# An expert's first weights used in two halves by all its passes, in the MoE of a transformer block

## The chip, the cores and the metric

One core of a Trainium2 chip. Its engines run side by side and meet at semaphores: TensorE (PE in the rows; PEld its weight loads, PEq its sequencer), VectorE (DVE), ScalarE (ACT), GpSimd (POOL), and SyncE (SP), which here mainly issues DMA transfers. PSUM is the memory that TensorE accumulates in, SBUF the working memory. The metric is device time of one execution in microseconds (us), lower is better.

## The reference

One streaming-encoder block on 256 tokens of width 1024: layer norm, one wide projection, a sparse latent attention and a state-space mixer, merged, and then a mixture of experts. All of the change lies in the last part:

```python
logits = (xt @ w_router + b_router)
top_val, top_idx = lax.top_k(logits, 4)            # 4 of 32 experts for each of 256 tokens
gates = jax.nn.softmax(top_val, axis=-1)
# for every expert e, for the tokens that chose it, with their gates g:
h = xt[tok] @ w1[e] + b1[e]                        # w1[e] is 1024 x 2048, float32
gate, up = h[:, :1024], h[:, 1024:]
gate = jnp.minimum(gate, 7.0); up = jnp.clip(up, -7.0, 7.0)
act = (up + 1.0) * gate * jax.nn.sigmoid(1.702 * gate)
acc.at[tok].add((act @ w2[e] + b2[e]) * g[:, None])   # w2[e] is 1024 x 1024
```

The 32 experts' weights are 384 MB in float32, all of them read once.

## The kernel before

The first quarter of the time goes to attention and mixer; from about 375 us on the kernel loops over the 32 experts (L1637 of the program). The order of instructions on each engine is the order in which the code is written.

**Weights.** An expert's weights are 12 units of 1 MB, eight of w1 (128 rows of 1024 each) and four of w2. They pass through a ring of 17 tiles (names wa, wb, wc; load_unit, L1014). SP issues the loads in order: load_more(8) after the block "a" of an expert and load_more(4) after its block "b". A load waits for the last matmul that reads the old contents of its tile, so when the ring is full it is TensorE that gives a tile back. The transfers are issued from one queue, in order.

**Slots and passes.** The tokens of an expert are numbered in slots. Pass 0 computes the first 32 slots for every expert; pass 1 the slots 32 to 63, pass 2 slots 64 to 127, pass 3 slots 128 to 191. Passes 1 to 3 stand in nested tc.If blocks on the number of tokens (if_more), which every engine branches around where they aren't needed (TensorE at L1508). With this input pass 1 runs in twelve experts (3, 6, 8, 10, 15, 16, 17, 21, 24, 27, 28, 30), pass 2 in experts 3, 15 and 17, and pass 3 in expert 15. `will` places a hint ahead of a branch for TensorE's instruction fetch.

**One expert.** Pass 0 takes its tokens from xg, gathered an expert pair ahead; its first product (first_bias and first_mm) goes through the eight w1 units into the PSUM tile X[0]. Then comes block "a": for each further pass the whole first product over the same eight units (more_first; passes 2 and 3 gather their own tokens with 32 matmuls into xo), swiglu on VectorE and ACT, one-hot matrices for the scatter (slots), and transposes (turn). Then the previous expert's outputs are scattered into acc (the list late), the next pair's tokens are gathered, pass 0's result is transposed, and its second product goes through the four w2 units into X[1] and Y[1]. Block "b" does the second product of the further passes (more_second) and scatters it: for each half of the columns ACT writes yh, the rounded scaled value, VectorE yl, the remainder, and eight matmuls add both into acc.

**Buffers.** go and so (swiglu of further passes), yh and yl of further passes, and some late scratch share a rotation of four tiles of 2 KB per partition (wide, tag t2k). h of a 64-slot pass lies in Y[0] and X[1].

In the last expert, w2 is loaded in column halves, and the residual and final layer norm follow each half.

Of the kernel before, what the change touches and what calls it, by code (L numbers as in the profile page):

```python
# [64 lines left out]
def shape_constants():  # L65
    p = np.arange(P)
    f32 = np.float32
    ident = np.eye(P, dtype=f32)
    tri = (p[:, None] <= p[None, :]).astype(f32)
    tgt = (p[:, None] > p[None, :]).astype(f32)  # L70
    trs = (p[:, None] < p[None, :]).astype(f32)
    iota = np.tile(np.concatenate([p % 32 + 1, p % 64 + 1, p + 1]).astype(f32)[None, :], (P, 1))
# [20 lines left out]
def kernel(ctx, tc, A, out, dbg=None):  # L93
# [43 lines left out]

    cst = const.tile([P, 672], F32, name="cst")
    nc.scalar.dma_start(cst[:, 0:128], A["cst"][:, 0:128])
# [261 lines left out]
    def small_b():  # L401
        small(cst2, A["cst"][:, 672:1184])
        small(cst3, A["cst"][:, 1184:1568])
        small(cst[:, 128:672], A["cst"][:, 128:672])
# [1020 lines left out]

    def first_mm(w, x, h, m, k):
        for c in range(4):
            t, j = h[c * m // P], c * m % P
            mm(t[j:j + m, :], lhsT=x[:, k, 0:m], rhs=w[:, :, c * 256:c * 256 + 256], start=False,  # L1429
               stop=(k == KD - 1), skip_group_check=True)  # L1430

    def turn(us, h, a):
        for i, u in enumerate(us):
            for c in range(2):
                tr(h[i][:, cut(c)], u[:, cut(c)], ident)
            act(a[:, i * 256:i * 256 + 256], h[i][:, 0:256], AF.Copy)  # L1436

# [11 lines left out]

    def scale_y(y, gs, tag=None):  # L1450
        v = [wide(nm, F32R) if tag else buf(nm, [512], F32R, 2) for nm in ("yh", "yl")]
        act(v[0], y, AF.Copy, scale=gs)  # L1452
# [21 lines left out]

    def own_gather(e, base):
        g = buf("hgo", [2, M])
        onehot(g, e, iota64[:, 0:M], base)
        gather(g, xo, 0, X[1], M)

    def more_first(e, p):  # L1480
# [12 lines left out]
        turn(us, h, aTs[p])  # L1493

    def more_second(e, p, nhs):
# [5 lines left out]
        for nh in nhs:  # L1501
            scatter(nh, more[e, p][0], scale_y(ys[nh], more[e, p][1], "t2k"))

# [11 lines left out]
    def rest(e, dw):  # L1515
        own_gather(e, FULL)
        sg = slots(e, put_hot(e, iota64, FULL, "o"), Y[1], "2", 1)
        h, a = (X[0], Y[0]), aTs[2]
        first_bias(e, h, M)
        for k in range(KD):  # L1520
            nc.sync.dma_start(dw, w1[e, cut(k), :])
            first_mm(dw.rearrange("p (g c) -> p g c", g=2), xo, h, M, k)
        turn([swiglu(t, True) for t in h], h, a)
        y = X[1], Y[1]
# [6 lines left out]
        for nh in range(2):  # L1531
            scatter(nh, sg[0], scale_y(y[nh], sg[1], "t2k"))

    def gate_values():
        for tt in range(2):
            m8 = rm8[:, tt, :]
            nm = buf("rnm", [4], bufs=2)
            V.tensor_scalar(nm[:, 0:1], m8[:, 0:1], -1.0, None, op0=OP.mult)
            ex = buf("rex", [NE], bufs=2)
            act(ex, l36[:, tt, 0:NE], AF.Exp, bias=nm[:, 0:1])  # L1540
# [4 lines left out]
        dump("gates", gates)  # L1545
        gr = buf("gr", [2, NE])
        V.tensor_copy(gp[:, :, :, 0], gates)
# [7 lines left out]
    def res(tt, hf, eng):  # L1555
        cs = slice(hf * 512, (hf + 1) * 512)
        tmp = wide("ftmp")
        V.tensor_tensor(tmp, acc[tt][hf], fin[0][:, cs], op=OP.mult)  # L1558
# [78 lines left out]
    for e in range(NE):  # L1637
# [113 lines left out]
```

## Time and profile before

| | before |
|---|---|
| median of 3 runs | 1521.28 us (1519.26 to 1521.94) |
| profiled execution, its own time | 1524.34 us |
| span of that execution in the trace | 1522.5 us |
| TensorE busy | 1225.6 us (80% of the span) |
| VectorE, ACT, POOL busy | 35%, 19%, 11% |
| mean granted TensorE clock | 0.905 of full |
| read from HBM | 475 MB |

The share of busy time is a mean over stretches that differ. A wait in the rows names what ended last before an instruction; an instruction's duration includes its overlap with its neighbours, since matmuls are pipelined.

### The profile page before, as it was taken

The numbers are of one execution on the slowest core, as the hardware profiler recorded it, in microseconds if no ns is written. First come the engines' busy times: TensorE is split into PE (matmuls) and PEld (weight loads), VectorE is DVE, ScalarE is ACT, GpSimd is POOL, SyncE is SP. The second block draws the span as 40 slices with busy tenths as digits, with TensorE's granted clock in tenths as the row PEclk, the third lists the DMA queues.
The fourth block names the chain that finished last, engine by engine and source line by source line (L and its number), as shares of the span: only waits on it lengthen the run. The fifth ranks groups of instructions, "written<-read, shape, count | busy, mean of one in ns | idle before, by whom it ended". The sixth has DMA issues, their size and how long they took to land. (4 is left out here: it accounts for less than half of the span.)

```text
span 1522.5 us, 21278 instructions
## 1 busy us (share of the span) xinstructions
PE 1225.6 (80%) x8399; PEld 666.2 (44%) x8399; DVE 537.1 (35%) x1107; ACT 294.1 (19%) x508; POOL 172.1 (11%) x123
## 2 busy tenths in 40 slices
PE   6988989998768878787777788988867777778784
PEld 3778778886323333334323243433332323323331
DVE  5678689786311212122212112221121212212134
ACT  2465546543100101010100001011000001001011
POOL 2333135423000000000000000000000000000002
PEclk9889989999978999899998869989998989989896
DMA  9777446987995699999999905465899999999971
GB/s 305 227 216 255 159 161 203 307 290 304 372 409 220 245 414 415 412 412 415 413 413 414 407 31 221 193 252 215 323 415 415 412 414 415 414 413 370 386 316 43
DMA packets 127430, 480.89 MB, mean 316 GB/s; under 512 B 12635, under 2 KB 49643, under 8 KB 92406
## 3 DMA queue, kind: packets, MB, share of 16 engines
q1 hardware_dynamic: 122598, 472.40, 79.3%
q10 hardware_dynamic: 4624, 5.67, 1.2%
q8 instruction: 137, 2.24, 0.6%
q14 instruction: 71, 0.58, 0.1%
HBM read 475.00 MB, written 3.03 MB: 314 GB/s over the span
## 5 line engine op out<-in xcount | busy, mean ns | idle before, releaser
L1429 PE MATMUL px<-wb,xg 128*32 128x512 f32 x1080 | 143.1, 646 | 28.4 <-DMA wb<-in_w 24.4
L1459 PE MATMUL acc<-yh,sT 128*128 128x512 f32 x192 | 95.4, 497 | 50.2 <-PEq L1508 39.5
L1395 POOL TENSOR_TENSOR xg<-xg,modT 128x512 f32<-128x512 f32 x32 | 33.3, 1040 | 875.9 <-DVE xg L1393 875.9
L1412 DVE TENSOR_SCALAR gu<-px 128x256 f32<-128x256 f32 x32 | 13.6, 425 | 303.5 <-PE px L1429 303.5
L426 PE MATMUL pj<-uTh,wl 128*128 128x256 f32 x360 | 106.9, 297 | 5.4 <-DVE wl L305 2.9
L426 PE MATMUL pj<-uTh,wh 128*128 128x256 f32 x360 | 108.6, 302 | 0.4 <-ACT iqz L645 0.4
L305 POOL TENSOR_TENSOR wl<-wa,wh 128x1024 fp32r<-128x1024 f32 x34 | 87.8, 2583 | 178.6 <-ACT wh L304 150.4
L426 PE MATMUL pj<-uTl,wh 128*128 128x256 f32 x360 | 106.4, 295 | 0.0
L1453 DVE SCALAR_TENSOR_TENSOR yl<-px,gs,yh 128x512 fp32r<-128x512 f32 x48 | 36.0, 751 | 198.1 <-ACT yh L1452 194.2
L304 ACT ACTIVATE wh<-wa 128x1024 fp32r<-128x1024 f32 x75 | 78.7, 1057 | 107.3 <-PE pj L426 77.7
L1459 PE MATMUL acc<-yl,sT 128*128 128x512 f32 x192 | 92.7, 483 | 4.5 <-DVEq L1508 3.1
L1414 ACT ACTIVATE sgm<-gu 128x256 f32<-128x256 f32 x32 | 13.3, 416 | 397.0 <-DVE gu L1412 397.0
L1459 PEld LDWEIGHTS acc<-yh,sT 128*128 128x128 f32 x192 | 43.6, 227 | 97.1 <-issue 54.1
L1429 PEld LDWEIGHTS px<-wb,xg 128*32 128x32 f32 x1080 | 34.6, 115 | 116.3 <-issue 68.4
L1443 PE MATMUL px<-wb,aT 128*32 128x512 f32 (+1 forms) x376 | 70.3, 600 | 17.0 <-ACT aT L1436 8.9
L1429 PE MATMUL px<-wa,xg 128*32 128x512 f32 x504 | 73.3, 685 | 11.4 <-DMA wa<-in_w 8.8
L1393 DVE TENSOR_TENSOR xg<-py,sc 128x512 f32<-128x512 f32 x32 | 22.1, 692 | 170.1 <-PE py L1389 99.0
L426 PEld LDWEIGHTS pj<-uTh,wl 128*128 128x128 f32 x360 | 72.6, 202 | 8.2 <-POOL wl L305 3.5
L1389 PEld LDWEIGHTS py<-hg,n 128*128 128x128 f32 x512 | 71.1, 213 | 11.2 <-issue 6.2
L426 PEld LDWEIGHTS pj<-uTh,wh 128*128 128x128 f32 x360 | 72.7, 202 | 4.0 <-issue 2.9
L1389 PE MATMUL py<-hg,n 128*128 128x128 f32 x512 | 69.8, 294 | 5.5 <-issue 2.5
L1429 PE MATMUL px<-wc,xg 128*32 128x512 f32 x464 | 62.8, 656 | 13.4 <-DMA wc<-in_w 13.4
(442 smaller groups left out, 2069.2 us busy)
## 6 DMA issues: line engine op xcount, KB each, us to landing
wb<-in_w SPq DMA_DIRECT2D x201, 1024.0 KB, 19.1
wc<-in_w SPq DMA_DIRECT2D x92, 1024.0 KB, 20.1
wa<-in_w SPq DMA_DIRECT2D x91, 1024.0 KB, 18.4
wa<-in_w_in SPq DMA_DIRECT2D x24, 1024.0 KB, 6.9
wa<-in_w_mod SPq DMA_DIRECT2D x16, 1024.0 KB, 5.0
wa<-in_w_mod SPq DMA_DIRECT2D x16, 512.0 KB, 6.1
wa<-in_w_proj_b SPq DMA_DIRECT2D x4, 1024.0 KB, 5.2
wa<-in_w_proj_a SPq DMA_DIRECT2D x4, 1024.0 KB
```

The source lines that it names most:

```text
L304: i = act(xh, x, AF.Copy)
L305: eng.tensor_tensor(xl, x, xh.bitcast(F32), op=OP.subtract)
L426: mm(o, lhsT=a[:, k, :], rhs=b[:, k, :], start=(k == 0 and i == 0), stop=(k == KD - 1 and i == 2), skip_group_check=True)
L1389: mm(t[:, i * m:(i + 1) * m], lhsT=n2[:, tt, cut(k0 + i)], rhs=oh[:, tt, :], start=(tt == 0), stop=(tt == 1), skip_group_check=True)
L1393: V.tensor_tensor(o, t.rearrange("p (a s) -> p a s", a=n), sc2[:, ks].unsqueeze(2).to_broadcast([P, n, m]), op=OP.mult)
L1395: G.tensor_tensor(o, o, sh2[:, ks].unsqueeze(2).to_broadcast([P, n, m]), op=OP.add)
L1412: V.tensor_scalar(gt, h[:, 0:w], SWIGLU_LIMIT, None, op0=OP.min)
L1414: act(sg, gt, AF.Sigmoid, scale=SWIGLU_ALPHA)
L1429: mm(t[j:j + m, :], lhsT=x[:, k, 0:m], rhs=w[:, :, c * 256:c * 256 + 256], start=False, stop=(k == KD - 1), skip_group_check=True)
L1443: mm(y[m * j:m * j + m, :], lhsT=a[:, b:b + m], rhs=w, start=(k < n), stop=(k >= KD - n), skip_group_check=True)
L1453: V.scalar_tensor_tensor(v[1], y, gs, v[0].bitcast(F32), op0=OP.mult, op1=OP.subtract)
L1459: mm(acc[tt][nh], lhsT=sT[:, tt, :], rhs=y, start=False, stop=False, skip_group_check=True)
```

## The change

w1 of an expert is used in two halves of four units. After pass 0's first four units comes a block "a0", in which every further pass goes over the same four; then load_more(4) gives SP those four tiles; then pass 0's last four units, a block "a1" with the further passes over them, and load_more(4). Pass 1 keeps its sums in its PSUM tile Y[0] between the blocks. The 64-slot passes share X[1] and Y[1], so they copy their sums of the first half into a new SBUF tile, part, and add it to the sums of the second half before swiglu. Each such pass keeps its gathered tokens (tiles xa2, xa3, later reused for the transposed result).

The rotation t2k is gone: go and so, and yho and ylo for the second product of all further passes, are single tiles; scratch of the end lies in part. hp, hg and sT of pass 0 go from two buffers to one. In the last expert pass 0's second product is scaled ahead of the branch, and the final rows are built after block "a1".

```diff
-    def wide(nm, dt=F32):
-        return buf(nm, [512], dt, 4, "t2k")
-
     def act_tiles(spare):
-        return (wide("go"), wide("so")) if spare else (buf("gu", [512]), buf("sgm", [256]))
+        return (buf("go", [512]), buf("so", [256])) if spare else (buf("gu", [512]), buf("sgm", [256]))
-    aTs = {1: buf("aT1", [256]), 2: buf("aT2", [512]), 3: buf("aT3", [512])}
-    xo = buf("xo", [KD, M])
+    aTs = {1: buf("aT1", [256]), 2: buf("xa2", [512]), 3: buf("xa3", [512])}
+    part = {2: buf("part2", [2, 512]), 3: buf("part3", [2, 512])}
+    yo = [buf(nm, [512], F32R) for nm in ("yho", "ylo")]
...
+    def more_first(e, p, q):
+        ks = range(4 * q, 4 * q + 4)
         if p == 1:
-            put = put_hot(e, iota32, T, "o")
-            x, h, m = xs(e)[:, :, T:M], (Y[0],), T
+            x, h, m, k0 = xs(e)[:, :, T:M], (Y[0],), T, -1
         else:
-            put = put_hot(e, iota64, LOW[p], "o")
-            own_gather(e, LOW[p])
-            x, h, m = xo, (Y[0], X[1]), M
-        first_bias(e, h, m)
-        for k in range(KD):
-            first_mm(wt[e * 12 + k], x, h, m, k)
-        us = [swiglu(t, True) for t in h]
-        more[e, p] = slots(e, put, Y[1], str(p), 1)
-        turn(us, h, aTs[p])
+            x, h, m, k0 = own(p), (X[1], Y[1]), M, 4
+            if q == 0:
+                own_gather(e, LOW[p], x)
+        if q == 0:
+            first_bias(e, h, m)
+        else:
+            put = put_hot(e, iota32 if p == 1 else iota64, LOW[p], "o")
+        for k in ks:
+            first_mm(wt[e * 12 + k], x, h, m, k, k0)
+        if p > 1:
+            v = [part[p][:, i, :] for i in range(2)]
+            if q == 0:
+                V.tensor_copy(v[0], h[0])
+                act(v[1], h[1], AF.Copy)
+            else:
+                for i in range(2):
+                    V.tensor_tensor(v[i], h[i], v[i], op=OP.add)
+        if q == 1:
+            for i, t in enumerate(h):
+                u = swiglu(v[i] if p > 1 else t, True)
+                if i == 0:
+                    more[e, p] = slots(e, put, Y[1], str(p), 1)
+                turn(u, X[1] if p > 1 else t, aTs[p], i)
...
-            scatter(nh, more[e, p][0], scale_y(ys[nh], more[e, p][1], "t2k"))
+            scatter(nh, more[e, p][0], scale_y(ys[nh], more[e, p][1], yo))
...
-        will(e, "a")
+        will(e, "a0_")
         first_bias(e, (h,), T)
         for k in range(KD):
             first_mm(wt[e * 12 + k], xs(e), (h,), T, k)
...
-        us = [swiglu(h)]
-        if_more(e, "a", more_first)
-        load_more(KD)
+            if k == 3:
+                if_more(e, "a0_", more_first, 0)
+                load_more(4)
+                will(e, "a1_")
+        u = swiglu(h)
+        if_more(e, "a1_", more_first, 1)
+        load_more(4)
...
             second_mm(w2_part(e, k, nh), y[nh], aT, T, k)
+        v = scale_y(y[nh], gs)
         will(e, "b%d_" % nh)
         if_more(e, "b%d_" % nh, more_second, (nh,))
-        scatter(nh, sT, scale_y(y[nh], gs))
+        scatter(nh, sT, v)
```

**Order of instructions.** TensorE, expert 0, from pass 0's units into the block for further passes; px_3648 is X[0] (pass 0), py_3650 Y[0] (pass 1), an x16 row four units. Before:

```order
L1429 MATMUL px_3648<-wb,xg 32x512 x16
L1429 MATMUL px_3648<-wa,xg 32x512 x16
L1508 COMPARE_AND_BRANCH
L1505 REGISTER_ALU
L1738 BRANCH_PREFETCH_HINT
L1423 LDWEIGHTS selc
L1423 MATMUL py_3650<-b1s,selc 32x512
```

Now, the entry into block "a0" at the same place, and then its end, pass 0's last four units and the entry into "a1":

```order
L1433 MATMUL px_3648<-wb,xg 32x512 x16
L1525 COMPARE_AND_BRANCH
L1522 REGISTER_ALU
L1762 BRANCH_PREFETCH_HINT
L1427 LDWEIGHTS selc
```

```order
L1525 UNCONDITIONAL_BRANCH x4
L1522 REGISTER_ALU
L1762 BRANCH_PREFETCH_HINT
L1433 MATMUL px_3648<-wa,xg 32x512 x16
L1525 COMPARE_AND_BRANCH
L1522 REGISTER_ALU
L1762 BRANCH_PREFETCH_HINT
L1433 MATMUL py_3650<-wa,xg 32x512 x16
```

There were eight units of pass 0, a branch, and eight of pass 1; now four of each stand on either side, with a second branch and hint between.

VectorE, expert 0, end of pass 2's first product in block "a"; xo is the gathered input, px_3649 X[1], py_3651 Y[1]. Before:

```order
L1393 TENSOR_TENSOR xo<-px_3649,sc_2716 128x512
L1412 TENSOR_SCALAR go<-py_3650 128x256
L1415 TENSOR_SCALAR go<-py_3650 128x256
L1416 SCALAR_TENSOR_TENSOR go<-go 128x256
L1417 TENSOR_TENSOR go<-go,so 128x256
L1412 TENSOR_SCALAR go<-px_3649 128x256
L1415 TENSOR_SCALAR go<-px_3649 128x256
L1416 SCALAR_TENSOR_TENSOR go<-go 128x256
L1417 TENSOR_TENSOR go<-go,so 128x256
L1405 CAST sT_3943<-py_3651 128x256
L1406 TENSOR_REDUCE gs_3944<-py_3651 128x1
```

Now, in block "a1", after the one-hots:

```order
L1504 TENSOR_TENSOR part_3681<-px_3649,part_3681 128x512
L1504 TENSOR_TENSOR part_3681<-py_3651,part_3681 128x512
L1416 TENSOR_SCALAR go<-part_3681 128x256
L1419 TENSOR_SCALAR go<-part_3681 128x256
L1420 SCALAR_TENSOR_TENSOR go<-go 128x256
L1421 TENSOR_TENSOR go<-go,so 128x256
L1409 CAST sT_4003<-py_3651 128x256
L1410 TENSOR_REDUCE gs_4004<-py_3651 128x1
L1416 TENSOR_SCALAR go<-part_3681 128x256
L1419 TENSOR_SCALAR go<-part_3681 128x256
L1420 SCALAR_TENSOR_TENSOR go<-go 128x256
L1421 TENSOR_TENSOR go<-go,so 128x256
```

Two adds into part stand ahead, and the cast and reduction of the slots have moved from behind both swiglu chains to between them.

ACT, expert 0, scaling of the second product in block "b", passes 1 and 2; the number after a name is its buffer. Before:

```order
L1508 COMPARE_AND_BRANCH
L1452 ACTIVATE yh_4130<-px1_3649,gs1_3855 128x512
L1452 ACTIVATE yh_4138<-py1_3651,gs1_3855 128x512
L1508 COMPARE_AND_BRANCH
L1452 ACTIVATE yh_4166<-px1_3649,gs2_3944 128x512
L1452 ACTIVATE yh_4174<-py1_3651,gs2_3944 128x512
```

Now:

```order
L1525 COMPARE_AND_BRANCH
L1455 ACTIVATE yho_3683<-px1_3649,gs1_3961 128x512
L1455 ACTIVATE yho_3683<-py1_3651,gs1_3961 128x512
L1525 COMPARE_AND_BRANCH
L1455 ACTIVATE yho_3683<-px1_3649,gs2_4004 128x512
L1455 ACTIVATE yho_3683<-py1_3651,gs2_4004 128x512
```

Each half had a buffer of its own; now all of them write one.

## Rows read from the trace of the kernel before

**Rows 1.** The page, parts 1 and 2 (GB/s: 40 slices of 38 us).

```profile
PE 1225.6 (80%) x8399; PEld 666.2 (44%) x8399; DVE 537.1 (35%) x1107; ACT 294.1 (19%) x508; POOL 172.1 (11%) x123
GB/s 305 227 216 255 159 161 203 307 290 304 372 409 220 245 414 415 412 412 415 413 413 414 407 31 221 193 252 215 323 415 415 412 414 415 414 413 370 386 316 43
```

**Rows 2.** Windows: length, busy us of each engine, TensorE clock, DMA share, GB/s.

```profile
530.00:841.00 311.00, 238.21 (x1752) 102.62 (x1744) 63.50 (x167) 28.68 (x56) 11.44 (x11) 0.93 1.02 413
841.00:860.00 19.00, 10.97 (x68) 1.72 (x72) 1.89 (x4) 0.58 (x2) 0.00 (x0) 0.76 1.01 413
860.00:1073.00 213.00, 187.65 (x1116) 83.09 (x1104) 45.39 (x119) 21.33 (x42) 6.25 (x6) 0.89 0.48 193
```

**Rows 3.** Waits of TensorE, 860 to 1073 us: total us, times, longest.

```profile
PE px L1429 <- DMA wb<-in_w: 1.3, 1, 1.3
```

**Rows 4.** Waits of TensorE, 530 to 860 us.

```profile
PE acc L1459 <- PEq L1508: 18.2, 8, 4.0
PE px L1429 <- DMA wb<-in_w: 14.9, 13, 1.7
PE px L1423 <- PEq L1508: 14.0, 10, 3.9
PE px L1429 <- DMA wc<-in_w: 6.8, 5, 1.8
```

**Rows 5.** Waits of TensorE, 1073 to 1342 us.

```profile
PE px L1429 <- DMA wb<-in_w: 7.1, 6, 1.8
PE px L1429 <- DMA wa<-in_w: 7.0, 8, 1.5
PE px L1429 <- DMA wc<-in_w: 4.3, 4, 1.5
```

**Rows 6.** Waits of TensorE, 841 to 860 us (expert 15, pass 0).

```profile
PE px L1429 <- DMA wb<-in_w: 8.0, 7, 1.7
```

**Rows 7.** Timeline of TensorE, expert 15: start, us, instruction, idle before.

```profile
848.28 1.93 PE L1429 MATMUL px<-wb,xg 128*32 128x512 f32 x8 [1.44 <-DMA wb<-in_w]
860.68 0.65 PE L1423 MATMUL py<-b1s,selc 96*32 96x512 bf16 x4
```

**Rows 8.** Timeline of TensorE, expert 4, pass 0.

```profile
527.89 5.33 PE L1429 MATMUL px<-wb,xg 128*32 128x512 f32 x48
```

**Rows 9.** Timeline of TensorE, expert 27.

```profile
1331.48 2.31 PE L1429 MATMUL px<-wa,xg 128*32 128x512 f32 x16
1343.43 0.65 PE L1423 MATMUL py<-b1s,selc 96*32 96x512 bf16 x4
```

**Rows 10.** Waits of TensorE, 1320 to 1343 us (expert 27, pass 0).

```profile
PE px L1429 <- DMA wc<-in_w: 2.0, 2, 1.4
PE px L1429 <- DMA wa<-in_w: 1.9, 2, 1.4
```

**Rows 11.** Waits of TensorE, 1342 us to the end.

```profile
PE acc L1459 <- ACTq L1508: 3.0, 4, 0.9
PE acc L1459 <- ACT yh L1452: 3.0, 1, 3.0
```

**Rows 12.** Timeline of all engines, expert 3, second product of pass 1.

```profile
514.44 0.69 ACT L1452 ACTIVATE yh<-py,gs 128x512 fp32r<-128x512 f32 x1 [1.03 <-PE py L1443]
514.82 0.40 PE L1459 MATMUL acc<-yh,sT 128*128 128x512 f32 x1
515.96 0.50 PE L1459 MATMUL acc<-yl,sT 128*128 128x512 f32 x1 [0.28 <-DVE yl L1453]
```

**Rows 13.** Groups of instructions by line: busy us, mean ns.

```profile
L1558 DVE TENSOR_TENSOR ftmp<-acc,wb 128x512 f32<-128x512 f32 x4 | 2.7, 683 | 1.8 <-PE acc L1459 1.8
```

**Rows 14.** Timeline of all engines, expert 3, end of pass 2's first product.

```profile
495.79 0.42 DVE L1412 TENSOR_SCALAR go<-px 128x256 f32<-128x256 f32 x1
495.93 0.44 PE L1435 MATMUL py<-cst,go 128*128 128x128 f32 x2 [1.19 <-DVE go L1417]
```

**Rows 15.** Timeline of TensorE, expert 3, pass 2's gather.

```profile
470.85 1.33 PE L1389 MATMUL px<-hgo,n 128*128 128x64 f32 x10 [0.52 <-DVE hgo L1381]
```

More of the change, by code (lines that the diff above doesn't have):

```diff
@@ L71, in shape_constants @@
     trs = (p[:, None] < p[None, :]).astype(f32)
-    iota = np.tile(np.concatenate([p % 32 + 1, p % 64 + 1, p + 1]).astype(f32)[None, :], (P, 1))
+    iota = np.tile(np.concatenate([p % 32 + 1, p % 64 + 1]).astype(f32)[None, :], (P, 1))
     fold = (p[:, None] % 32 == np.arange(32)[None, :]).astype(f32)
@@ L136 @@
     b_mod = A["b_mod"][0]
-    cst = const.tile([P, 672], F32, name="cst")
+    cst = const.tile([P, 544], F32, name="cst")
     nc.scalar.dma_start(cst[:, 0:128], A["cst"][:, 0:128])
@@ L401, in small_b @@
     def small_b():
-        small(cst2, A["cst"][:, 672:1184])
-        small(cst3, A["cst"][:, 1184:1568])
-        small(cst[:, 128:672], A["cst"][:, 128:672])
+        small(cst2, A["cst"][:, 544:1056])
+        small(cst3, A["cst"][:, 1056:1440])
+        small(cst[:, 128:544], A["cst"][:, 128:544])
         small(kvw, bcast_rows(A["kv_norm_w"][0], P))
@@ L1364, in buf, with own, half @@
         return mp.tile([P] + shape, dt, name=nm, tag=tag or nm, bufs=bufs)
-    def wide(nm, dt=F32):
-        return buf(nm, [512], dt, 4, "t2k")
     def act_tiles(spare):
-        return (wide("go"), wide("so")) if spare else (buf("gu", [512]), buf("sgm", [256]))
+        return (buf("go", [512]), buf("so", [256])) if spare else (buf("gu", [512]), buf("sgm", [256]))
     aT = buf("aT", [256])
-    aTs = {1: buf("aT1", [256]), 2: buf("aT2", [512]), 3: buf("aT3", [512])}
-    xo = buf("xo", [KD, M])
+    aTs = {1: buf("aT1", [256]), 2: buf("xa2", [512]), 3: buf("xa3", [512])}
+    part = {2: buf("part2", [2, 512]), 3: buf("part3", [2, 512])}
+    yo = [buf(nm, [512], F32R) for nm in ("yho", "ylo")]
+    def own(p):
+        return aTs[p].rearrange("p (k s) -> p k s", k=KD)
+    def half(i):
+        return part[2 + i // 2][:, i % 2, :]
     b1v = b1s.rearrange("p (g c) -> p g c", g=2)
@@ L1424, in first_bias, with first_mm, turn @@
                start=True, stop=False, skip_group_check=True)
-    def first_mm(w, x, h, m, k):
+    def first_mm(w, x, h, m, k, k0=-1):
         for c in range(4):
             t, j = h[c * m // P], c * m % P
[L1429 to L1436, printed above, removed]
+            mm(t[j:j + m, :], lhsT=x[:, k, 0:m], rhs=w[:, :, c * 256:c * 256 + 256], start=(k == k0),
+               stop=(k == KD - 1 or k + 1 == k0), skip_group_check=True)
+    def turn(u, h, a, i=0):
+        for c in range(2):
+            tr(h[:, cut(c)], u[:, cut(c)], ident)
+        act(a[:, i * 256:i * 256 + 256], h[:, 0:256], AF.Copy)
     def second_mm(w, y, a, m, k):
@@ L1448, in w2_part, with scale_y @@
         return wt[e * 12 + KD + nh * 2 + k // 4][:, k % 4, :]
-    def scale_y(y, gs, tag=None):
-        v = [wide(nm, F32R) if tag else buf(nm, [512], F32R, 2) for nm in ("yh", "yl")]
+    def scale_y(y, gs, v=None):
+        v = v or [buf(nm, [512], F32R, 2) for nm in ("yh", "yl")]
         act(v[0], y, AF.Copy, scale=gs)
@@ L1515, in rest @@
     def rest(e, dw):
-        own_gather(e, FULL)
+        own_gather(e, FULL, own(2))
         sg = slots(e, put_hot(e, iota64, FULL, "o"), Y[1], "2", 1)
@@ L1521, in rest @@
             nc.sync.dma_start(dw, w1[e, cut(k), :])
-            first_mm(dw.rearrange("p (g c) -> p g c", g=2), xo, h, M, k)
-        turn([swiglu(t, True) for t in h], h, a)
+            first_mm(dw.rearrange("p (g c) -> p g c", g=2), own(2), h, M, k)
+        for i in range(2):
+            turn(swiglu(h[i], True), h[i], a, i)
         y = X[1], Y[1]
@@ L1531, in rest @@
         for nh in range(2):
-            scatter(nh, sg[0], scale_y(y[nh], sg[1], "t2k"))
+            scatter(nh, sg[0], scale_y(y[nh], sg[1], yo))
     def gate_values():
@@ L1538, in gate_values @@
             V.tensor_scalar(nm[:, 0:1], m8[:, 0:1], -1.0, None, op0=OP.mult)
-            ex = buf("rex", [NE], bufs=2)
+            ex = half(3)[:, tt * NE:(tt + 1) * NE]
             act(ex, l36[:, tt, 0:NE], AF.Exp, bias=nm[:, 0:1])
@@ L1545, in gate_values @@
         dump("gates", gates)
-        gr = buf("gr", [2, NE])
+        gr = half(2)[:, 0:2 * NE].rearrange("p (a b) -> p a b", a=2)
         V.tensor_copy(gp[:, :, :, 0], gates)
@@ L1556, in res @@
         cs = slice(hf * 512, (hf + 1) * 512)
-        tmp = wide("ftmp")
+        tmp = half(2 * tt + hf)
         V.tensor_tensor(tmp, acc[tt][hf], fin[0][:, cs], op=OP.mult)
@@ L1653 @@
                     scatter(*v)
-                for i in range(3):
-                    for hf in range(2):
-                        fin_row(i, hf, (X[1], Y[1])[hf])
-        us = [swiglu(h)]
-        if_more(e, "a", more_first)
-        load_more(KD)
+            if k == 3:
[5 more added lines that the diff above has]
+        load_more(4)
+        if last:
+            for i in range(3):
+                for hf in range(2):
+                    fin_row(i, hf, (X[1], Y[1])[hf])
         if not last:
@@ L1665 @@
                 pair_gather(q, e % 2)
-        sT, gs = slots(e, put, Y[1], "", 2)
-        turn(us, (h,), aT)
+        sT, gs = slots(e, put, Y[1], "", 1)
+        turn(u, h, aT)
         if not last:
@@ L1685 @@
         if e == NE - 3:
-            gTs = wide("gTs")[0:32, :]
+            gTs = half(0)[0:32, :]
             b2s = wt["b2"]
```

12 lines of the change are left out of this document (5 added, 7 removed).

## Prediction

> **What bounds the kernel now.** I began with the page: TensorE is busy 80% of the span, and the row of GB/s by slice is flat near 414 in the expert loop except in the six slices from 875 to 1103 us, where it falls to between 31 and 323 [rows 1]. Neither engine nor memory bounds the kernel all the way, so I cut the loop into stretches and read each apart [rows 2]: from 530 to 841 us the DMA engines are full (413 GB/s), from 860 to 1073 they move 193 GB/s, and TensorE is busy 187.65 of 213 us. The slices show the DMA full again from 1103 to about 1340 us. Then I asked in each stretch what TensorE waits for. From 860 to 1073 it waits 1.3 us for weights [rows 3]: the DMA is idle there because the ring is full of weights not yet used, not the other way round. From 530 to 860 it waits 21.7 us for weights (14.9 + 6.8), beside 32.2 us for its own sequencer at the branches of L1508 (18.2 + 14.0, in 18 waits, 1.8 us each on average) [rows 4]; from 1073 to 1342 it waits 18.4 us for weights [rows 5]. After 1342 weights are not among its waits, which are for ACT, VectorE and branches.
>
> So an earlier release lets a transfer start earlier, but from 860 to 1073 us nothing waits for one; and at 1073 the ring is full whatever happened before, because its last four units, expert 17's w2, are given back by that expert's last pass in both versions. What the halves can gain lies where TensorE comes out of a DMA-bound stretch into an expert with more passes: it can do a second pass over the four units at hand while the other four are landing. Such places are expert 15 (from 841 us), expert 27 (from 1327 us) and, weakly, expert 3.
>
> **The change part by part.**
>
> Entry into expert 15. Before, pass 0 waits on seven units, 8.0 us in all [rows 6]; its fourth unit begins at 848.28 and takes 1.93 us, and pass 1 starts at 860.68, after the eighth [rows 7]. Now pass 1 starts after the fourth, at 850.2: 10.5 us earlier. Four units of pass 0 are then still to do; six take 5.33 us where nothing delays them [rows 8], so four take 3.55. Gain 10.5 - 3.55 = 6.9 us; more than the 8.0 us of waits can't come back.
>
> Entry into expert 27. Four units are done at 1333.8 (1331.48 + 2.31), and pass 1 started at 1343.43, after the eighth [rows 9]. By the rule of expert 15 that is 9.65 - 3.55 = 6.1 us, but the eighth unit still lands when it did and four units of pass 1 must follow it. The four waits for weights between are 3.9 us (2.0 + 1.9) [rows 10], which I take; bounds 2 and 6.1.
>
> Experts 0 to 3. The first slots come free a little earlier, but experts 0 to 2, which skip, now skip once more each (1.8 us by [rows 4]). I take -1 us, between -3.5 and +3.2.
>
> Last expert. Its second output is now scaled ahead of the branch. Before, TensorE waited 3.0 us for that scaling (ACT yh) [rows 11]; VectorE and ACT came late to it for other reasons too, the residual's statistics among them, so I take 0.85 us, bounds 0 and 3.0.
>
> Gains together: 6.9 + 3.9 + 1 + 0.85 = 12.65 us.
>
> One pair yho, ylo for the second product of the extra passes. Before, ACT writes the second half's yh at 514.44, while the scatter of the first half is still being read, and the second half's first matmul on yl starts at 515.96 [rows 12]. Now it is the same buffer: ACT must wait for the third matmul of the scatter, yh's last reader, which ends at 514.82 + 0.40 = 515.22. It starts near 515.3, and what follows moves by 0.85 to 0.9 us. TensorE has nothing else to do: the next pass's second product is queued behind this scatter. The extra passes in stretches that TensorE bounds are 3 in expert 15, 1 in 16, 2 in 17, 2 in 3, and 1 each in 27, 28 and 30: 11 x 0.9 = 9.9 us (bounds 5, if semaphores of before are absorbed, and 11). In experts 6, 8, 10, 21 and 24 it lies under the DMA.
>
> The 64-slot passes (expert 3, 15 twice, 17: four). Their first product now ends with two VectorE adds of 128x512 from PSUM, 0.68 us each as the same shape takes in L1558 [rows 13], the second of them behind the last matmul. Then come the two halves of swiglu. Before, the second began at 495.79, ahead of the transposes that read the first (495.93, 0.44 us) [rows 14]; now go is one buffer, so the second must wait for them, and the cast and reduction of the slots stand between. 0.75 for the add, 0.5 to 0.7 for the transposes, 0.5 for cast and semaphores: 1.85 us each, 7.4 in all (bounds 4 and 10). The copies into part after the first half (0.7 us on VectorE and ACT) lie beside pass 0's other four units, except in expert 15, where pass 3's gather writes X[1] next: +0.75. Against that, pass 2's gather no longer follows pass 1's transposes, where it waited 0.52 us for its one-hots [rows 15]: -0.5 x 3 = -1.5.
>
> The second If around w1. Where it is taken and the next pass skipped (experts 3, 15, 16, 17, 27, 28, 30) its join costs what those of before cost: 3.0 us over four (ACTq), 0.75 each [rows 11], so 7 x 0.75 = 5.3 (bounds 3 and, at 1.8, 12.6). Where it is skipped in the last stretch (29, 31) I take the mean, 2 x 1.8 = 3.6. In the two DMA-bound stretches eight and seven skipping experts pay 1.8 too, and the experts with a pass 1 pay 0.75 + 0.9: 8 x 1.8 + 3 x 1.65 = 19.4 us, against 21.7 - 8.0 = 13.7 us of weight waits ahead of expert 15; 7 x 1.8 + 2 x 1.65 = 15.9 against 18.4 - 3.9 = 14.5 ahead of expert 27. TensorE so comes to expert 15 some 5.7 us later and still finds its fourth unit landing at 848; I cost them at nothing, but this cover is then used up.
>
> Pools cut from two buffers to one (hp, hg, sT): their writers are an expert ahead of their readers; nothing taken, bound 3 us.
>
> Costs: 9.9 + 7.4 + 0.75 - 1.5 + 5.3 + 3.6 = 25.45 us. Net +12.8 us on 1524.34, the time of the profiled execution. It stands 0.2% above the median, to which I add the same: 1521.28 + 12.8 = 1534.
>
> **A rule weighed against the rows.** From 860 to 1073 us the DMA moves 193 GB/s and TensorE waits 1.3 us for it [rows 2, 3]. The Trainium skill, "Perfetto Trace Analysis", section Optimization Strategy, says that the same gap, repeating on the engine that should be saturated, can mean there isn't enough SBUF for the next tile. By that rule, read on the DMA, giving slots back early would bring back up to 213 x (1 - 193/413) = 113 us; by the row the engine that should be saturated is TensorE, and nothing of it comes back.
>
> **The rivals.**
>
> The give-back pays and the costs hide (faster). Gains at their bounds are 8.0 + 6.1 + 3.5 + 3.0 = 20.6 us, costs at theirs 5 + 4 + 0.75 - 1.5 + 3 + 2 = 13.25: 1514. It decides if the wait of yho is less than half of what I take and the joins hide. For it: TensorE's granted clock is 0.76 from 841 to 860 [rows 2], and could be higher with work in place of waits. Against: the added instructions stand where TensorE has nothing else.
>
> No change: gains of 15 to 20 meet costs of 15 to 20, 1521 +- 3.
>
> The skips miss (much slower). A branch stalls TensorE by up to 4.0 us [rows 4]. At 2.9 us on average the DMA-bound stretches need 8 x 2.9 + 5 = 28 us against 21.7, and 7 x 2.9 + 3.3 = 23.6 against 18.4: +6 and +5, +2 in the last stretch, and the gains at experts 15 and 27 fall by some 5: 1552. At 3.9 it is 1565. For it: each hint now stands four units ahead of its branch instead of eight. Against: the code that one If skips is shorter.
>
> The Trainium skill, "Runtime: NRT & Kernel Launch", section Instruction fetch mechanics, states that a taken branch whose target isn't among the pages at hand forces a fetch before execution goes on. By that rule this rival would hold wherever a block is skipped; the trace agrees that such waits are there, 18 of them in 330 us, with the mean of 1.8 us that my sum uses.
>
> **How the numbers follow.** Forecast 0.52 (its own range 1526 to 1543), skips miss 0.20, faster 0.15, no change 0.13. Some 0.2%, 3 us, is what a measurement of this kernel can tell from no change. The range leaves out the far ends of the first and the third rival: 1517 to 1550. Faster 0.15, same 0.13, slower 0.72.
>
> **What would show it.** The pause of the DMA after 875 us stays, with weight waits near 1 us in it. Expert 15's pass 1 starts ten us before its eighth unit of pass 0, and its weight waits shrink from 8.0 to about 2. ACT's second yho begins after the third matmul of the scatter, and TensorE waits near 1 us there. In the DMA-bound stretches waits at the branches rise by half and weight waits fall as much. The prediction is too low if those weight waits vanish, too high if the second scatter shows no wait, and off either way if the granted clock from 860 to 1073, 0.89 now, moves by over 0.03.

## The result

The changed kernel takes 1576.06 us (median of 4 runs, 1566.57 to 1581.69), the kernel before 1520.27 (1515.88 to 1521.94): a ratio of 1.0365, 95% interval 1.0305 to 1.0425, 3.65% slower. The forecast was 1534, the range ended at 1550; the sign was right and the size wrong. The profiled execution took 1566.57 us, with a span of 1564.8. It is the fastest of the four, so the trace holds 42 of the 56 us.

Page of the changed kernel: busy time by engine, GB/s by slice (39 us each), and instruction fetches (queue q8: packets, MB).

```profile
PE 1223.6 (78%) x8399; PEld 664.5 (42%) x8399; DVE 540.8 (35%) x1119; ACT 296.7 (19%) x512; POOL 173.1 (11%) x123
GB/s 311 232 226 248 162 142 247 347 287 317 414 376 202 209 412 414 413 364 413 344 412 413 350 152 106 288 178 155 414 412 411 357 414 402 411 376 302 409 237 28
q8 instruction: 161, 2.64, 0.7%
```

And the last of these rows in the kernel before:

```profile
q8 instruction: 137, 2.24, 0.6%
```

TensorE does the same matmuls in the same busy time (1225.6 before, [rows 1]), and the DMA still pauses, now in the slices from about 900 to 1095 us. The 42 us are time in which TensorE is idle, and 24 more packets of instructions were fetched. To see where, I cut both traces at the first bias matmul of the same experts: 0 to 3, 4 to 14, 15, 16 and 17, 18 to 26, 27, 28 to the end. Windows of the kernel before (length, busy us of PE, PEld, DVE, ACT, POOL, clock, DMA share, GB/s):

```profile
375.40:527.70 152.30, 118.44 (x779) 50.97 (x778) 36.50 (x102) 15.23 (x29) 6.24 (x6) 0.88 0.74 299
527.70:841.10 313.40, 240.56 (x1776) 103.50 (x1780) 63.56 (x168) 28.78 (x56) 11.44 (x11) 0.93 1.02 413
841.10:963.80 122.70, 103.62 (x540) 42.77 (x540) 23.68 (x63) 10.46 (x21) 3.12 (x3) 0.85 0.50 201
963.80:1073.90 110.10, 94.96 (x637) 41.99 (x636) 24.20 (x64) 11.35 (x22) 3.12 (x3) 0.92 0.55 220
1073.90:1327.70 253.80, 192.34 (x1402) 82.44 (x1405) 51.69 (x135) 22.95 (x44) 9.37 (x9) 0.91 1.02 412
1327.70:1376.30 48.60, 37.83 (x244) 14.35 (x245) 9.13 (x25) 4.25 (x8) 1.04 (x1) 0.81 1.02 414
1376.30:1522.50 146.20, 107.20 (x740) 42.43 (x740) 44.10 (x90) 17.40 (x32) 10.02 (x9) 0.86 0.69 273
```

The same experts in the changed kernel:

```profile
370.50:528.70 158.20, 116.31 (x779) 49.41 (x778) 38.05 (x105) 17.17 (x31) 6.25 (x6) 0.89 0.72 288
528.70:864.00 335.30, 248.20 (x1772) 107.60 (x1773) 63.49 (x168) 28.72 (x56) 11.44 (x11) 0.90 0.99 399
864.00:974.40 110.40, 94.13 (x540) 39.71 (x540) 26.77 (x69) 11.82 (x23) 3.12 (x3) 0.94 0.48 189
974.40:1090.30 115.90, 96.43 (x641) 41.93 (x640) 25.74 (x67) 12.00 (x23) 3.12 (x3) 0.93 0.52 207
1090.30:1368.60 278.30, 196.51 (x1398) 84.65 (x1399) 49.80 (x132) 22.43 (x44) 9.37 (x9) 0.90 1.00 402
1368.60:1407.90 39.30, 31.36 (x244) 13.64 (x244) 11.01 (x29) 4.77 (x9) 1.04 (x1) 0.96 0.93 378
1407.90:1564.80 156.90, 113.57 (x740) 43.68 (x740) 44.01 (x90) 17.41 (x32) 10.03 (x9) 0.83 0.62 244
```

Experts 4 to 14 take 21.9 us more and 18 to 26 24.5 us more: these are the DMA-bound stretches, in which the prediction costed the second If at nothing. Experts 15 and 27, the entries, take 12.3 and 9.3 less. Each stretch taken with its entry, it is 9.6 us more for experts 4 to 15 and 15.2 for 18 to 27. DMA falls from 413 to 399 and from 412 to 402 GB/s in the two stretches: the weights are no longer the bound.

Waits of TensorE in experts 4 to 14 of the changed kernel:

```profile
PE acc L1462 <- PEq L1525: 19.2, 8, 5.4
PE px L1427 <- PEq L1525: 15.9, 9, 4.0
PE px L1433 <- PEq L1525: 13.3, 8, 3.7
PE px L1433 <- issue: 9.2, 4, 3.7
PE px L1433 <- DMA wb<-in_w: 4.2, 2, 3.8
```

Before, the sequencer's first two rows were 18.2 and 14.0 us [rows 4], much the same; the third row (13.3 us at L1433, the fifth unit of pass 0, right behind a0) is new, and so is over half of the fourth (4.2 us before). The weight waits fall from 15.6 us (the part of [rows 4] that lies ahead of expert 15, with 1.8 us on wa) to 6.1, the last row and 1.9 us on wa. One expert that needs no further pass shows it (expert 5, TensorE's timeline; in such rows a unit is x8):

```profile
557.22 2.92 PE L1433 MATMUL px<-wb,xg 128*32 128x512 f32 x16
560.60 1.06 PE L1433 MATMUL px<-wb,xg 128*32 128x512 f32 x8 [0.46 <-PEq L1525]
565.33 4.48 PE L1433 MATMUL px<-wb,xg 128*32 128x512 f32 x24 [3.66 <-issue]
571.80 0.49 PE L1462 MATMUL acc<-yh,sT 128*128 128x512 f32 x1 [1.99 <-PEq L1525]
```

The third and fourth unit of pass 0 end at 560.1. The fifth begins after 0.46 us, the sixth 3.66 us after the fifth has ended, at 565.33, without a wait for weights; and behind a1 the scatter waits another 1.99 us. In the trace's list of DMA packets one of q8 lands at 563.91, 1.4 us before the sixth unit begins.

In experts 18 to 26 the waits for the sequencer and those for nothing that the profile shows rise by 22.0 us, while the weight waits hardly fall, from 14.5 to 11.8; most of that is now three long waits:

```profile
PE px L1433 <- DMA wb<-in_w: 11.1, 3, 4.2
```

One term of the sum, in expert 15:

```profile
PE acc L1462 <- ACT yho L1455: 1.6, 3, 0.6
```

### The profile page after: what moved, and what is told of

Read it like the earlier page. It is cut to its first block, busy times and chain, and to the rows that moved or that the text cites. A ratio compares the mean times of both kernels' runs of the same rounds, so it can differ in the third digit from the quotient of the medians.

```text
span 1564.8 us, 21828 instructions
## 1 busy us (share of the span) xinstructions
PE 1223.6 (78%) x8399; PEld 664.5 (42%) x8399; DVE 540.8 (35%) x1119; ACT 296.7 (19%) x512; POOL 173.1 (11%) x123
## 5 line engine op out<-in xcount | busy, mean ns | idle before, releaser
L1433 PE MATMUL px<-wb,xg 128*32 128x512 f32 x1080 | 151.6, 687 | 41.0 <-PEq L1525 24.1
L1462 PE MATMUL acc<-yh,sT 128*128 128x512 f32 x128 | 69.8, 546 | 55.6 <-PEq L1525 41.7
L1418 ACT ACTIVATE sgm<-gu 128x256 f32<-128x256 f32 x32 | 13.3, 417 | 446.1 <-DVE gu L1416 446.1
L1433 PEld LDWEIGHTS px<-wb,xg 128*32 128x32 f32 x1080 | 39.8, 123 | 136.0 <-issue 124.5
L1433 PE MATMUL px<-wa,xg 128*32 128x512 f32 x504 | 71.8, 670 | 19.6 <-DMA wb<-in_w 8.6
L1397 DVE TENSOR_TENSOR xg<-py,sc 128x512 f32<-128x512 f32 x32 | 22.1, 692 | 179.4 <-PE py L1393 97.9
L1433 PE MATMUL px<-wc,xg 128*32 128x512 f32 x464 | 70.4, 721 | 12.1 <-DMA wb<-in_w 6.8
L1446 PE MATMUL px<-wb,aT 128*32 128x512 f32 x348 | 62.2, 610 | 17.1 <-ACT aT L1439 8.9
L1456 DVE SCALAR_TENSOR_TENSOR yl<-px,gs,yh 128x512 fp32r<-128x512 f32 x32 | 24.0, 751 | 148.0 <-ACT yh L1455 143.0
L425 PEld LDWEIGHTS pj<-uTl,wh 128*128 128x128 f32 x360 | 71.6, 199 | 1.2 <-issue 0.8
L1462 PEld LDWEIGHTS acc<-yh,sT 128*128 128x128 f32 x128 | 32.3, 253 | 86.9 <-issue 58.2
## 6 DMA issues: line engine op xcount, KB each, us to landing
wa<-in_w SPq DMA_DIRECT2D x91, 1024.0 KB, 13.1
```

The source lines that it names most:

```text
L425: mm(o, lhsT=a[:, k, :], rhs=b[:, k, :], start=(k == 0 and i == 0), stop=(k == KD - 1 and i == 2), skip_group_check=True)
L1397: V.tensor_tensor(o, t.rearrange("p (a s) -> p a s", a=n), sc2[:, ks].unsqueeze(2).to_broadcast([P, n, m]), op=OP.mult)
L1418: act(sg, gt, AF.Sigmoid, scale=SWIGLU_ALPHA)
L1446: mm(y[m * j:m * j + m, :], lhsT=a[:, b:b + m], rhs=w, start=(k < n), stop=(k >= KD - n), skip_group_check=True)
L1456: V.scalar_tensor_tensor(v[1], y, gs, v[0].bitcast(F32), op0=OP.mult, op1=OP.subtract)
L1462: mm(acc[tt][nh], lhsT=sT[:, tt, :], rhs=y, start=False, stop=False, skip_group_check=True)
```

## The experiments

Theory S: every expert that needs no further pass pays a second jump around skipped code, whose target TensorE has to fetch; in the DMA-bound stretches that uses up the slack and makes TensorE the bound. Rivals: B, the buffers cut to one and the sums in SBUF slow every expert; R, SP issues late, because load_more is split by branches. Two later theories are on the hints that will places ahead of a branch: L, a skip is cheap only if its hint stands far enough ahead of it; H, the hint for a0 sets off a fetch of its own, which delays the one for a1. Each ratio below is to the kernel before, run on the same chip.

| run | median us | ratio, 95% interval | instruction packets on q8 |
|---|---|---|---|
| before | 1520 to 1523 | | 137 |
| changed | 1576.06 | 1.0365 (1.0305 to 1.0425) | 161 |
| x1 a0 where needed | 1504.01 | 0.9888 (0.9830 to 0.9947) | 122 |
| x2 before plus skip | 1598.83 | 1.0510 (1.0448 to 1.0571) | 183 |
| x3 a0 for pass 1 only | 1543.32 | 1.0118 (1.0044 to 1.0192) | 152 |
| x4 If and Else | 1538.42 | 1.0102 (1.0049 to 1.0155) | 152 |
| x6 no weight loads | 1415.69 (one run) | | 161 |
| x7 before, hint later | 1520.87 | 0.9986 (0.9967 to 1.0005) | 138 |
| x8 x1, release undone | 1504.17 | 0.9876 (0.9849 to 0.9902) | 122 |
| x9 x3, hint early | 1517.42 | 0.9952 (0.9926 to 0.9977) | 141 |
| x10 x9, two pairs | 1509.70 | 0.9881 (0.9842 to 0.9921) | 141 |
| x11 x3, no a0 hint | 1538.93 | 1.0095 (1.0065 to 1.0125) | 152 |
| x12 changed, no a0 hint | 1562.22 | 1.0241 (1.0200 to 1.0281) | 161 |
| x13 x12, a1 hint early | 1551.56 | 1.0177 (1.0146 to 1.0208) | 159 |

**x1: block a0 only where it is used.** NEED lists the further passes of the twelve experts that have any.

```diff
     def if_more(e, nm, f, *a, p=1):
+        top = NEED.get(e, 0) if nm == "a0_" else 3
+        if p > top:
+            return
...
-        will(e, "a0_")
+        if e in NEED:
+            will(e, "a0_")
```

> The changed kernel, but block a0 is only written for the experts and passes that use it with this input (for other inputs it would leave passes out); everything else of the change stays. Theory S (the 20 skipping experts pay TensorE about 3 us each for the second branch, and in the two DMA-bound stretches this makes TensorE the bound): 1515 to 1530 us, weight waits of TensorE back near 15 to 20 us in each of the two stretches. Theory B (the pools cut to one buffer, yho, go and the sums in SBUF make every expert slower): 1560 to 1580, as the changed kernel. Theory R (the split release and the added branches keep SP from issuing in time): 1560 to 1580, since SP's load_more calls stay split.

1504 us, 72 less than the changed kernel and 16 to 19 less than the one before: below the range that S gave. B falls: all buffers and sums are still in it. So does R as far as the split release goes; the needless branches are gone for SP too, but the waits that went are those for TensorE's own sequencer. Windows of experts 0 to 3, 4 to 14, 15, 18 to 26 and 27:

```profile
370.20:510.80 140.60, 110.69 (x778) 48.21 (x778) 37.90 (x105) 17.15 (x31) 6.23 (x6) 0.93 0.81 323
510.80:828.60 317.80, 246.84 (x1772) 106.38 (x1771) 65.74 (x174) 29.24 (x56) 11.42 (x11) 0.90 1.02 412
828.60:939.90 111.30, 95.05 (x544) 39.68 (x544) 24.60 (x63) 11.27 (x22) 3.12 (x3) 0.92 0.52 209
1053.20:1303.70 250.50, 195.29 (x1402) 85.25 (x1401) 49.88 (x133) 22.42 (x44) 9.35 (x9) 0.90 1.02 413
1303.70:1346.30 42.60, 31.79 (x248) 12.02 (x248) 10.99 (x29) 4.75 (x9) 1.04 (x1) 0.96 1.02 415
```

Experts 4 to 14 run at 412 GB/s again, and expert 15 still takes 11.4 us less than before, expert 27 6.0 less. In both TensorE's busy time falls, 103.62 to 95.05 and 37.83 to 31.79 us, at a clock of 0.92 and 0.96 instead of 0.85 and 0.81. But in the stretches ahead of them it rises, by 6.3 and 3.0 us, at a lower clock (0.90 instead of 0.93 and 0.91), and experts 4 to 14 take 4.4 us more. Each entry taken with its stretch, 4 to 15 takes 7.0 us less than before and 18 to 27 9.3 less. TensorE at the two entries in x1, expert 15 and then expert 27:

```profile
828.64 0.62 PE L1427 MATMUL px<-b1s,selc 96*32 96x512 bf16 x4 [3.90 <-PEq L1529]
829.03 1.94 PE L1433 MATMUL px<-wc,xg 128*32 128x512 f32 x8
830.74 3.34 PE L1433 MATMUL px<-wb,xg 128*32 128x512 f32 x24
833.90 0.39 PE L1427 MATMUL py<-b1s,selc 96*32 96x512 bf16 x4
```

```profile
1311.87 0.65 PE L1427 MATMUL py<-b1s,selc 96*32 96x512 bf16 x4
1320.15 1.06 PE L1433 MATMUL px<-wc,xg 128*32 128x512 f32 x8 [1.23 <-DMA wc<-in_w]
```

In expert 27 the halves do what they are for: pass 1 starts 8.3 us ahead of pass 0's eighth unit, which TensorE still waits for. In expert 15 TensorE comes off a wait of 3.9 us for its sequencer and goes through the first four units without a wait for weights, so no overlap with a transfer is seen there.

The largest difference to the kernel before lies elsewhere, in experts 0 to 3: 11.7 us. There, and in all skipping experts, x1 skips block a1, with four units' matmuls, in place of block a, with eight, and the waits behind the skip, over the whole span, are a third of the 39.5 us of before. In the changed kernel, with the same a1 and an a0 jump ahead of it, they are three times as long. First x1, then the changed kernel behind a1 and behind a0:

```profile
PE acc L1462 <- PEq L1529: 13.1, 19, 3.2
```

```profile
PE acc L1462 <- PEq L1525: 41.7, 19, 5.5
PE px L1433 <- PEq L1525: 36.7, 23, 5.3
```

So the jumps around a0 cost 36.7 us behind themselves and 28.6 more behind a1, 65 in all. The spans of the two traces differ by 64, though other waits and TensorE's busy time changed as well.

**x2: the kernel before with a jump more.** 92 matmuls with their weight loads are jumped over, as in a0. The new jump's hint stands ahead of pass 0, where block a's stood; block a's moves behind the new jump.

```diff
+    def never(e):
+        with tc.If(counts[e] > 250, label="x%d_1" % e):
+            first_bias(e, (Y[0],), T)
+            for k in range(4):
+                first_mm(wt[e * 12 + k], xs(e)[:, :, T:M], (Y[0],), T, k)
+            for p in (2, 3):
+                own_gather(e, LOW[p])
+                first_bias(e, (Y[0], X[1]), M)
+                for k in range(4):
+                    first_mm(wt[e * 12 + k], xo, (Y[0], X[1]), M, k)
...
+            if k == 3:
+                never(e)
+                will(e, "a")
```

> The kernel before with one more tc.If after the fourth unit of every expert's pass 0, never taken (more than 250 tokens), around as much TensorE code as block a0 has (248 rows), with a hint like the others. Nothing else changes. Theory S: 1545 to 1570 us, branches of over 1 us about double from 530 to 860. Theories B and R: 1517 to 1526, no change.

1599 us, more than expected: a jump that does nothing costs more than the whole change. Its waits over the whole span, first those behind the new jump, then those behind block a (39.5 us in the kernel before, in 19 waits):

```profile
PE px L1429 <- PEq L1496: 82.4, 29, 5.6
PE acc L1459 <- PEq L1519: 54.5, 20, 5.9
```

The new jump costs 2.8 us each time, and the next one is dearer (54.5), though its hint has moved too. Windows of experts 4 to 14, 15 and 27:

```profile
532.60:877.40 344.80, 248.98 (x1776) 108.69 (x1778) 64.03 (x168) 29.23 (x56) 11.43 (x11) 0.89 0.95 381
877.40:989.20 111.80, 94.26 (x540) 40.22 (x540) 23.12 (x63) 9.96 (x20) 3.12 (x3) 0.94 0.52 205
1385.40:1425.20 39.80, 31.90 (x248) 13.36 (x248) 10.27 (x28) 4.24 (x8) 1.04 (x1) 0.96 1.02 412
```

Experts 15 and 27 take 10.9 and 8.8 us less than before, without any halves. So the same decrease in the changed kernel needs no halves: TensorE arrives late and finds its weights landed.

**x3, x4: fewer or shorter jumps.** x3 leaves passes 2 and 3 whole in a1 (release by load_more(8) after it), x4 puts a0, the last four units of pass 0 and a1 into one arm, and the four units again into the other.

```diff
-                if_more(e, "a0_", more_first, 0)
-                load_more(4)
+                with tc.If(counts[e] > LOW[1], label="a0_%d_1" % e):
+                    more_first(e, 1, 0)
...
```

> The changed kernel with only pass 1 halved: a0 jumps over 40 TensorE rows instead of some 250; passes 2 and 3 run whole in a1, without sums in SBUF, and the release goes back to load_more(8) after a1. Theory S, where the price is the fetch of a target that is far off: 1520 to 1540 us. Theory S with a price for any branch, however short: 1560 to 1580. Theory B (pools and yho are as in the changed kernel): 1555 to 1575.

```diff
...
+        with tc.If(counts[e] > LOW[1], label="a%d_1" % e) as cmp:
+            will(e, "a0_", 2)
+            more_first(e, 1, 0)
+            if_more(e, "a0_", more_first, 0, p=2)
+            will(e, "a1_", 2)
+            tail()
+            more_first(e, 1, 1)
+            if_more(e, "a1_", more_first, 1, p=2)
+        with cmp.Else():
+            tail()
+        load_more(KD)
```

> The changed kernel with one branch around w1 in place of two: if pass 1 is needed, a0, pass 0's last four units and a1 in one arm; otherwise pass 0's last four units in the other arm. load_more(8) behind it. An expert that needs pass 0 alone jumps as often as in the kernel before. Theory S: 1512 to 1535 us. Theory B: 1555 to 1575.

Both come out a little above what was expected, below the changed kernel and above the one before. In x3 the short a0 costs next to nothing (second row), but the waits behind a1 have doubled against the 39.5 us of block a:

```profile
PE acc L1462 <- PEq L1515: 85.4, 23, 6.3
PE px L1433 <- PEq L1663: 9.2, 19, 0.9
```

In x4 the jump into the other arm is charged as a wait for nothing that the profile shows, 3.3 us in each of the 20 experts that need pass 0 alone:

```profile
PE px L1433 <- issue: 66.4, 20, 4.8
```

**x6: no weight loads.**

```diff
+        if i >= 15:
+            t = raw[i % 15]
...
+            return
```

> The changed kernel without the weight loads behind the fifteenth unit: all later units read the first fifteen tiles again, so the expert loop has next to no DMA traffic (weights of other experts are not used). Everything else, all branches too, stays. Theory F1 (an instruction fetch takes about 6 us because it shares the DMA engines with the 1 MB loads): branches of TensorE over 1 us, 50 in the changed kernel, fall below 15, and TensorE's waits of 36.7 us behind a0 below 15. Theory F2 (a fetch takes that long by itself): both stay, 40 or more branches over 1 us.

Neither. Branches of over 1 us, counted in the trace from 365 us on, were 24 before and 54 in the changed kernel (the 50 of the expectation); here there are 42, so they don't vanish. But none is over 5 us, where the changed kernel has 27, and all branches together take 143 us instead of 283. The waits behind a0 fall from 36.7 to 22.1 us:

```profile
PE px L1446 <- PEq L1538: 22.1, 30, 3.0
```

So a jump costs TensorE something on an idle DMA, and about twice as much beside the 1 MB loads. That the price is a fetch, the traces' lists of DMA packets show: in the changed kernel 53 of the 54 branches over 1 us have a packet of q8 landing within them (a median of 1.4 us before the branch ends), and 1 of the 125 shorter ones; before, 24 of 24 and 0 of 96. The packet takes 1.1 us with or without the loads; what differs is how long after the branch's start it begins, a median of 3.0 us in the changed kernel and 0.9 in x6. Experts 4 to 14 take 268.6 us with the same jumps:

```profile
514.30:782.90 268.60, 222.81 (x1774) 96.39 (x1775) 63.59 (x168) 28.71 (x56) 11.43 (x11) 0.97 0.01 4
```

**x7, x9, x11: the hint.** x7 moves block a's hint in the kernel before from ahead of pass 0 to behind its fourth unit; x9 moves a1's hint in x3 the other way and drops a0's; x11 only drops a0's.

```diff
-        will(e, "a0_")
+        will(e, "a1_")
...
-                will(e, "a1_")
```

> The kernel before with one line moved: the hint for block a stands after pass 0's fourth unit instead of ahead of its first. Theory L (a skip is cheap if its hint comes far enough ahead): 1530 to 1550 us, waits at the scatter behind a skipped block a 60 us or more instead of 39.5. Without L: 1517 to 1527 and 35 to 45 us.

> The run with only pass 1 halved (1543 us), where the hint for the long block a1 is placed ahead of pass 0 as in the kernel before, and the short block a0 (40 instructions of TensorE) has none. Theory L: 1505 to 1522 us, waits behind a1 near 40 us instead of 85. If the place of the hint doesn't matter: 1538 to 1550.

> The run with only pass 1 halved (1543 us) without the hint for the short block a0; the hint for a1 stays behind a0, four units ahead of its branch. Theory H (a hint for a0 sets off a fetch of its own, and the fetch for a1 then comes too late): 1512 to 1525 us, waits behind a1 near 30 to 40 us, some 140 instruction packets. Theory L (the distance of a1's hint): 1538 to 1550, as that run, with 85 us.

Waits behind block a or a1 over the whole span, in x7, x9 and x11:

```profile
PE acc L1459 <- PEq L1508: 38.6, 19, 3.9
```

```profile
PE acc L1462 <- PEq L1515: 29.0, 19, 6.3
```

```profile
PE acc L1462 <- PEq L1515: 67.1, 19, 6.4
```

In the kernel before the place of the hint is worth nothing (L fails there). With a short jump ahead of it, it is worth 22 us (x11 against x9), and 11 packets fewer are fetched; a0's own hint is worth 4 us in x3 (x3 against x11), no more than the noise (H fails there). Why the place of the hint counts only where another jump stands between the two places stays open.

**x12, x13: the changed kernel with other hints.** x12 drops a0's hint, x13 also puts a1's ahead of pass 0.

> The changed kernel without the hint for a0. Theory S with H: each skip of a0 still needs its target fetched, unhinted, but a1's is no longer late: 1540 to 1570 us. If hints do nothing here: 1570 to 1580. If the hint for a0 is the whole price: 1505 to 1520.

> The changed kernel without the hint for a0 and with the hint for a1 ahead of pass 0. Theory S with H: between 1530 and 1565 us, below the run without a0's hint by up to 15 if the distance of a1's hint counts; the same as that run if it doesn't.

Both lie where S with H and L together put them: 14 us for a0's hint, 11 for the distance of a1's. The waits don't show how: TensorE's three rows of waits for its sequencer come to 121.1 us in the changed kernel, 128.7 in x12 and 127.8 in x13, so the cause of these gains stays open. The jump over a0 is still paid, in x13:

```profile
PE px L1433 <- PEq L1525: 53.6, 30, 5.4
PE acc L1462 <- PEq L1525: 31.8, 18, 5.4
```

**x8: the release undone in x1.** load_more(8) stands after a1 instead of 4 and 4.

> The run with a0 only where needed (1504 us), with the four units of the first half given back late: load_more(8) after a1 instead of 4 and 4. Theory of the entry (what is gained is that a further pass runs while pass 0's last units land): 1500 to 1512 us. Theory of the give-back (transfers that start earlier): 1518 to 1530, the gain over the kernel before gone.

1504.17 against 1504.01: giving the first four units back early shows no gain. What x1 gains is the entries and the cheaper skips; no run takes the two apart.

**x10: two pairs.** In x9 each half of the second product gets its own pair; the room comes from part3, whose scratch at the end moves to xa2 and xa3.

```diff
-    yo = [buf(nm, [512], F32R) for nm in ("yho", "ylo")]
+    yo = [[buf(nm + str(i), [512], F32R) for nm in ("yho", "ylo")] for i in range(2)]
...
-            scatter(nh, more[e, p][0], scale_y(ys[nh], more[e, p][1], yo))
+            scatter(nh, more[e, p][0], scale_y(ys[nh], more[e, p][1], yo[nh]))
```

> The run with only pass 1 halved and the hint early (1517 us), with a pair yho, ylo of its own for each half of the second product, as the kernel before had. By the waits of the trace (0.5 us on ACT yho in each of 16 further passes, 11 of them where TensorE is the bound): 1510 to 1516 us. If the pair mattered as much as the prediction says (0.9 us each): 1507 to 1511. If not at all: 1517.

1509.70 us, 0.9881 of the kernel before (0.9842 to 0.9921). It holds for any input and is 1.2% faster than the kernel before. 7.7 us between the medians of x9 and x10, 11 by their ratios, lies within the range for 0.9 us a pass and just past the one for 0.5; x9's runs spread over 14 us, so the size is not measured well. Expert 15 in x10:

```profile
841.90:958.80 116.90, 98.23 (x540) 43.09 (x540) 24.66 (x63) 10.75 (x21) 3.22 (x3) 0.90 0.52 206
```

It takes 116.9 us where x1, which halves the 64-slot passes too, takes 111.3.

## Why the prediction was wrong

**The step that failed** is the second If in the two DMA-bound stretches: "I cost them at nothing, but this cover is then used up". Measured, they take 21.9 and 24.5 us more, 9.6 and 15.2 when the entries behind them are counted in, where TensorE's lateness saves waits; and x1, which removes only the needless a0, gives back 72 us over the whole.

Two things were off in it. The price: without the scatter's 0.9 a pass, the sum had 16.7 us of jumps and joins in experts 4 to 14 and 14.1 in 18 to 26. The waits for the sequencer rose by 16.2 us in the first (18.2 + 14.0 before, 19.2 + 15.9 + 13.3 now) and those that the profile can't name by 5.0, 21.2 together; in the second it was 22.0. The mean of the skips of before, 1.8 us, was too low for a jump that follows another by four units: with the same a1, the waits behind it are 41.7 us in the changed kernel and 13.1 in x1. And the experts with a pass 1 were given 0.75 us for their join, though their a0 jumps over passes 2 and 3 too: those branches took 3.5, 3.9 and 5.5 us in experts 6, 8 and 10.

The larger error was the cover, which was taken as whole: of 15.6 us of weight waits in experts 4 to 14 only 9.5 went, and of 14.5 in 18 to 26 only 2.7. TensorE's busy time, which the sum left out, rose by 7.6 and 4.2 us, at a clock of 0.90 instead of 0.93 and 0.91.

**The rival that skips miss**, given 0.20, was the right mechanism, and still too small. At 2.9 us it gave 1552; at 3.9 the same sum gives about 1570, not the 1565 that stands there. That the gains at experts 15 and 27 would fall was wrong, as the lateness saved waits there, and the last stretch came out 10.7 us longer, not 8. The Trainium skill, "Runtime: NRT & Kernel Launch", section Instruction fetch mechanics, has the rule that carried it, that a taken branch to a page not at hand forces a fetch; x2 agrees, with 2.8 us a jump and 46 packets more.

**The reading of the bounds** was right: the pause of the DMA stayed, and x8 shows no gain from the release. Of the signs named, the clock was one of being off: in the stretch that was 860 to 1073 us before, it went from 0.89 to 0.93.

**The entries.** With their costs, expert 15 was to come out even and expert 27 2.3 us shorter. In x1 they are 11.4 and 6.0 us shorter, 7.0 and 9.3 with the stretches ahead of them. In expert 27 the mechanism is the one forecast, but the weight waits that I took as the gain are still there (4.4 us, 3.9 before). In expert 15 they are gone, but there TensorE came late, as in x2. I counted waits and left out the clock: 8.6 of the 11.4 us and all of the 6.0 are TensorE's busy time, of which 2.3 and 3.1 us are left once the stretches ahead are counted in. In the changed kernel itself 12.3 and 9.3 us are saved there, but x2 saves nearly as much by lateness alone.

**The costs on TensorE's path** came out near in sum: experts 16 and 17 were to take some 5.6 us more and took 5.8. The terms were not measured one by one, and the pair yho, ylo, priced 0.9 us a pass, shows 1.6 us over three in expert 15, so part of this may be luck.

**Experts 0 to 3** were, with the costs in expert 3, to lose 2.9 us and lost 5.9. Against x1, which has no a0 in experts 0 to 2, it is 17.6 us: the three needless jumps were priced far too low there as well, and the cheaper skip of a1 that hid half of it was not foreseen. The last four experts were to lose 6 and lost 10.7.

## What to carry to other kernels

A block that is skipped at run time isn't free on an engine whose code streams past it: count the jumps, look at what the skips of before already cost and at the packets on the instruction queue, and price the next one above the mean if it follows closely. Slack of a DMA-bound stretch is a sum to be spent once; when the spending comes near to it, forecast a new bound and not zero. Read an entry to a TensorE-bound stretch together with the stretch ahead of it: what TensorE comes late there, it doesn't wait here, and a lower busy time in the one can stand against a higher one in the other. An earlier release was worth nothing where the ring was full (x8).

## What the runs showed that was not expected

The time follows the number of instruction packets: from 122 (1504 us) to 183 (1599) it is some 1.6 us for each, and of the other kernels that load the weights none lies more than 25 us off that line. It is no more than a guide: the changed kernel and x12 both fetch 161 packets and lie 14 us apart. A jump costs about half where the DMA is idle (143 us of branches against 283). TensorE's granted clock in expert 15 is 0.85 in the kernel before, with 8.0 us of weight waits at its entry, and 0.92 to 0.94 in x1, x2 and the changed kernel, with less than 2, so the same 540 matmuls take 103.62 or 94 to 95 us. The waits alone don't set it: x10 has 6.4 us of them at 0.90, x3 1.8 us at 0.88.
